# The opening and the closing of a one-core decoder layer: identity made on GpSimd, packed vectors on ScalarE's queue, large scalings and transposes behind the first rows, output as four pieces on two queues

## The chip, the cores and the metric

The kernel runs on one core of one Trainium2 chip. The metric is the device time of one execution in microseconds, the median of several runs. Engines are called as in the profile: PE (TensorE), DVE (VectorE), ACT (ScalarE), POOL (GpSimd) and SP (SyncE, which here does nothing but issue transfers). Transfers are also issued on ACT's queue.

## The reference, cut to what matters

One decoder layer on 256 tokens of width 1024, with weights in float32. The opening is the first half-FFN: a modulation vector comes from `c`, the rows of `x` are normed and modulated, and go through the gate and up projections.

```python
c_act = silu(c)
mod = c_act @ w_ada + b_ada                      # 1024 x 9216
sh1, sc1, g1, sh2, sc2, g2, sh3, sc3, g3 = split(mod, 9)
u = rmsnorm(x, norm_ff1) * (1 + sc1) + sh1
h = x + 0.5 * g1 * ((silu(u @ w_ff1_gate) * (u @ w_ff1_up)) @ w_ff1_down)
...                                              # token mixing (GLA and MoBA), second half-FFN
return rmsnorm(h, norm_final)                    # 256 x 1024
```

## The kernel before, in words

Each float32 product is made of three passes: weights and rows are both split into a high part (`hi`, `uh`: rounded by an ACT copy) and the remainder (`lo`, `ul`: a DVE subtraction), and hi*hi, hi*lo and lo*hi are added in PSUM. A matmul here is 128 x 128 weights against 256 tokens. All weights (140 MB) stream through eight raw buffers of 128 x 1024, issued on SP's queue in the order of use; a load waits for the release of a raw buffer by DVE, and each transfer counts on one of eight completion semaphores that are taken in turn, so that a transfer also waits for the eighth before it.

The opening works on eight blocks k of 128 input features. For each block come two pieces of the modulation weights (`a`, from `adal`) and two of the first eight columns of gate and up (`l`, from `lead`). What it does for block k, by the letters of the string `LEADING` (line 27), which is the order of program on every engine:

- `d`: a dot product of a modulation piece with `cact` on DVE (about 1.2 us), which gives the shift or the scale of block k
- `e`: ACT copies two turned blocks of x from PSUM to `xn`
- `u`, `c`, `v`: the modulated rows, their high part `uh` (ACT), their low part `ul` (DVE), both in the tile `ub`
- `h`, `r`: the high part of a weight piece (ACT) and its remainder (DVE)
- `x`: the 24 matmuls of a block with one of its two weight pieces

So blocks 0 and 1 together are 96 matmuls. Ahead of that stand, in program order: loads of the packed vectors `colt` (line 273, SP's queue), of x in two halves (line 276) and of the identity `ident` (line 279, ACT's queue); `csil` = silu(c) on ACT; eight transposes that spread `csil` over all partitions, and their two copies to `cact`; warm-up transposes of the identity (`keep_warm`, 22, and 8 and 7 later, by `WARM`); the squares of x (1024 and 512 wide on ACT, 512 on DVE), the mean, and the power -1/2 on POOL; then the scaling of x by it in pieces of 256 and 768 columns per half (`s`, `lead_scaled`), and the transposes of x (`t`, `lead_turned`), 4 for the first two blocks and 12 for the others, all of them ahead of the first matmul (line 690).

The constants of the token mixing (`mask`, `onehot`, `relt`, `wlr`, three of `tri`) and the transposed copy `xT` are written down later in the program (`mix_constants`, line 712, and line 736); a scheduler decides where their loads stand in SP's queue.

At the end the normed result is transposed (16 transposes into four PSUM banks), scaled by the inverse root mean square on its way out of PSUM, and written: five pieces, four transfers on SP's queue and one on ACT's (lines 1170 to 1173).

Of the kernel before, what the change touches and what calls it, by code (L numbers as in the profile page):

```python
# [11 lines left out]
F32R = mybir.dt.float32r  # L12
# [11 lines left out]
WARM = (22, 8, 7)  # L24
LOADS = """a00 a01 l00 l01 a10 a11 l10 l11 a20 a21 l20 l21 a30 a31 l30 l31 a40 a41 l40 l41 a50 a51 l50 l51 a60
         a61 l60 l61 a70 a71 l70 l71"""
LEADING = """u0 c0 h00 v0 r00 e1 h01 e2 e3 d10 r01 d11 h10 u1 c1 r10 v1 d20 h11 r11 x00 x01 d21 h20 u2 c2 r20 v2
# [48 lines left out]
def hybrid_layer(ctx: ExitStack, tc: tile.TileContext, x, xT, cols, ident_d, tri_d, mask_d, onehot_d,  # L76
# [196 lines left out]
    nc.sync.dma_start(colt, cols)  # L273
# [5 lines left out]
    nc.scalar.dma_start(ident, ident_d)  # L279
# [9 lines left out]
    in_order(True, vec, act, ten)  # L289
    csil = cst.tile([P, KD], F32, name="csil")  # L290
# [10 lines left out]
    pc = [bank(), bank()]  # L301
# [3 lines left out]
    warm = bank()  # L305

    def keep_warm(n):

        for _ in range(n):
            ten.transpose(warm[:, :P], ident, ident)  # L310

    keep_warm(WARM[0])

    sq, ssq = [mid([P, D]), mid([P, D])], row((P, 8), tag="tiny", bufs=4)
    act.activation(sq[0], xt[:, 0:D], AF.Square, accum_out=ssq[:, 0:1])
    act.activation(sq[1][:, 0:512], xt[:, D:D + 512], AF.Square, accum_out=ssq[:, 1:2])
# [299 lines left out]
    def lead_mm(k, w):  # L616
# [68 lines left out]
    def lead_xn(i):  # L685
# [7 lines left out]
    play(LEADING, {"d": lead_dot, "u": lead_u, "c": lead_uh, "v": lead_ul, "h": lead_high, "r": lead_low,  # L693
                   "e": lead_xn, "x": lead_mm, "A": stream.more})
# [587 lines left out]
```

## Time and profile before

| | |
|---|---|
| time, median of 3 runs | 568.15 us (567.98 to 568.35) |
| the profiled execution | 568.44 us, its span 566.7 us |
| PE busy | 556.5 us (98% of the span), 4757 matmuls |
| DVE busy | 442.1 us (78%) |
| ACT busy | 304.5 us (54%) |
| POOL busy | 10.8 us (2%) |
| mean granted clock of PE | 0.998 |

The span runs from the first to the last instruction of the profiled execution; the time is 1.74 us longer. Times below are microseconds from the start of the span. A row of the timeline merges instructions of one kind that follow each other: start, the time they took together, engine, line, operation, out<-in, shape, count, and in brackets the idle time of the engine before it and what ended it. Almost all instructions go through one recording helper and carry its line, L101, so they are told apart by the names of what they read and write. In those names `b` is a PSUM bank or the large buffer that holds x; `tiny` holds the mean and its inverse root; `raw` is a weight as loaded. Ends of matmuls are modelled.

### The profile page before, as it was taken

What the parts mean: (1) busy time and instruction counts of PE and PEld (TensorE: products, weight loads), DVE (VectorE), ACT (ScalarE), POOL (GpSimd) and SP (SyncE); (2) the same over time, 40 slices, a digit from 0 to 9 for tenths busy, and PEclk for the clock granted to TensorE, in tenths of its full rate; (3) what the DMA queues carried; (4) which work ended last, traced back from release to release, by engine and by line L of the source; (5) the groups of instructions that cost most, each with busy time, mean ns of one, the idle gap of its engine ahead of it and who ended that gap; (6) DMA issues with size and microseconds to landing.
All of it is one profiled execution on the core that took longest, in us unless ns stands there. A gap on an engine that the chain in (4) does not pass through costs nothing.

```text
span 566.7 us, 11731 instructions
## 1 busy us (share of the span) xinstructions
PE 556.5 (98%) x4757; PEld 550.1 (97%) x4757; DVE 442.1 (78%) x683; ACT 304.5 (54%) x484; POOL 10.8 (2%) x14
## 2 busy tenths in 40 slices
PE   7999999999999999999999999999999999999996
PEld 6999999999999999998999999999999999999995
DVE  5999888788887896899998979789874656665535
ACT  5557763354455667843864543576644454455424
POOL 0000000000000110000001000000000000000000
PEclk9999999999999999999999999999999999999999
DMA  8999789999998636454499788834896566775102
GB/s 320 401 408 408 250 274 377 407 385 345 300 387 296 216 106 225 156 183 150 121 313 381 256 284 282 283 128 120 265 360 218 191 199 216 260 246 178 56 1 74
DMA packets 39799, 142.03 MB, mean 251 GB/s; under 512 B 4621, under 2 KB 5186, under 8 KB 39618
## 3 DMA queue, kind: packets, MB, share of 16 engines
q1 hardware_dynamic: 39282, 140.44, 71.2%
q8 instruction: 37, 0.61, 0.4%
q0 software_dynamic: 176, 0.53, 0.3%
q10 hardware_dynamic: 288, 0.33, 0.2%
q14 instruction: 16, 0.13, 0.1%
HBM read 140.22 MB, written 1.05 MB: 249 GB/s over the span
## 4 chain that ended last, share of the span: by engine, by line
PE 59%; issue 32%; DVE 5%; DMA 2%; ACT 1%; POOL 0%; SPq 0%; POOLq 0%; DVEq 0%
PE b L101 59%; DVE lo L101 2%; DMA raw<-in_lead 1%; DVE b L101 1%; DVE s L101 1%; DMA b<-in_x 1%; DVE raw L101 0%; POOL tiny L361 0%; ACT b L101 0%; ACT hi L101 0%; POOLq L1277 0%; DVEq L1277 0%; ACT ub L101 0%; DVE tiny L101 0%; SPq L276 0%
## 5 line engine op out<-in xcount | busy, mean ns | idle before, releaser
L101 PE MATMUL b<-ub,hi 128*128 128x256 f32 (+1 forms) x1920 | 329.9, 278 | 0.3 <-DVE ub L101 0.3
L101 PEld LDWEIGHTS b<-ub,hi 128*128 128x128 f32 x1920 | 288.6, 188 | 1.9 <-issue 1.0
L101 DVE TENSOR_TENSOR lo<-raw,hi 128x1024 fp32r<-128x1024 f32 (+2 forms) x189 | 225.4, 1218 | 65.8 <-ACT hi L101 64.6
L101 PE MATMUL b<-ub,lo 128*128 128x256 f32 (+1 forms) x960 | 262.4, 277 | 0.0
L101 ACT ACTIVATE hi<-raw 128x1024 fp32r<-128x1024 f32 (+2 forms) x189 | 193.8, 1049 | 69.9 <-issue 32.0
L101 PEld LDWEIGHTS b<-ub,lo 128*128 128x128 f32 x960 | 178.9, 188 | 0.0
L101 PE MATMUL b<-s,hi 128*128 128x256 f32 x960 | 164.6, 276 | 0.0
L101 PEld LDWEIGHTS b<-s,hi 128*128 128x128 f32 x960 | 144.7, 188 | 0.0
L101 PE MATMUL b<-s,lo 128*128 128x256 f32 x480 | 132.7, 276 | 0.0
L101 PEld LDWEIGHTS b<-s,lo 128*128 128x128 f32 x480 | 90.1, 188 | 0.0
L101 DVE SCALAR_TENSOR_TENSOR raw<-raw,cact 128x1024 f32<-128x1024 f32 (+1 forms) x64 | 75.9, 1221 | 0.0
L101 ACT ACTIVATE s<-m 128x256 fp32r<-128x256 f32 x52 | 21.4, 417 | 77.9 <-DVE m L101 77.8
L101 ACT ACTIVATE sg<-b 128x256 f32<-128x256 f32 x46 | 17.1, 379 | 47.8 <-PE b L101 45.9
L101 DVE TENSOR_TENSOR s<-m,s 128x256 fp32r<-128x256 f32 x52 | 21.8, 424 | 20.6 <-ACT s L101 20.3
L101 DVE TENSOR_TENSOR m<-sg,b 128x256 f32<-128x256 f32 x43 | 17.9, 418 | 13.5 <-ACT sg L101 13.4
L101 ACT ACTIVATE s<-b 128x256 f32<-128x256 f32 (+5 forms) x34 | 14.5, 474 | 25.1 <-PE b L101 22.0
L101 PE MATMUL b<-hi,ub 128*128 128x264 f32 (+1 forms) x96 | 21.7, 321 | 0.0
L101 PEld LDWEIGHTS b<-hi,ub 128*128 128x128 f32 x96 | 15.8, 188 | 1.2
L101 PE MATMUL b<-lo,ub 128*128 128x264 f32 (+1 forms) x48 | 15.4, 321 | 0.0
L101 DVE SCALAR_TENSOR_TENSOR b<-b,mods,b 128x256 f32<-128x256 f32 x24 | 10.6, 479 | 4.5 <-PE b L101 4.5
L361 POOL TENSOR_TENSOR tiny<-tiny,mhalf 128x2 f32<-128x2 f32 (+1 forms) x5 | 7.1, 1418 | 364.4 <-DVE tiny L101 364.4
L101 ACT ACTIVATE sq<-b 128x256 f32<-128x256 f32 x24 | 9.2, 407 | 5.6 <-DVE b L101 5.2
(124 smaller groups left out, 278.7 us busy)
## 6 DMA issues: line engine op xcount, KB each, us to landing
raw<-in_gu SPq DMA_DIRECT2D x72, 512.0 KB, 5.7
raw<-in_ada SPq DMA_DIRECT2D x56, 512.0 KB, 6.2
raw<-in_dn SPq DMA_DIRECT2D x44, 512.0 KB, 6.1
raw<-in_win SPq DMA_DIRECT2D x24, 512.0 KB, 4.8
raw<-in_adal SPq DMA_DIRECT2D x16, 513.0 KB, 8.2
raw<-in_lead SPq DMA_DIRECT2D x16, 512.0 KB, 8.0
raw<-in_gbr SPq DMA_DIRECT2D x16, 512.0 KB, 6.1
raw<-in_wout SPq DMA_DIRECT2D x8, 512.0 KB, 6.1
```

Of the source, the lines that this page charges most:

```text
L101: x = getattr(self.engine, op)(*args, **kw)
L361: nc.gpsimd.tensor_tensor(out=rs[:, :n], in0=ms[:, :n], in1=mhalf[:, :n], op=ALU.pow)
```

## The change

The identity is no longer loaded: GpSimd clears it and a select on the diagonal sets the ones; DVE casts a second copy, `ident_r`, to fp32r. The packed vectors go to ACT's queue. Warming up is now a plain matmul of `ident_r` with itself, 10 ahead of the transposes of `csil` and 24 behind them, and nothing later. ACT squares both halves of x whole. Ahead of the first matmul remain the two small scalings, four transposes and one copy to `xn`; the large scalings (`s11` on DVE, `s01` on ACT) and the 12 transposes (`t11`, `t01`) move into `LEADING`, behind the 16 matmuls of block 0 that need only the high part of the weights (`x00`); its 8 matmuls with the remainder follow as `y00`. The eight accumulation banks are handed out in another order. The output is two pieces of 512 columns per half, one on each queue. In the excerpt a line of three dots marks what is left out.

```diff
-WARM = (22, 8, 7)
+WARM = (10, 24)
...
-LEADING = """u0 c0 h00 v0 r00 e1 h01 e2 e3 d10 r01 d11 h10 u1 c1 r10 v1 d20 h11 r11 x00 x01 d21 h20 u2 c2 r20 v2
+LEADING = """u0 c0 s11 h00 v0 r00 x00 s01 t11 t01 y00 h01 e1 e2 e3 d10 r01 d11 h10 u1 c1 r10 v1 d20 h11 r11 x01 d21 h20 u2 c2 r20 v2
...
-    nc.sync.dma_start(colt, cols)
+    nc.scalar.dma_start(colt, cols)
...
-    nc.scalar.dma_start(ident, ident_d)
+    nc.gpsimd.memset(ident, 0.0)
+    nc.gpsimd.affine_select(out=ident, in_=ident, pattern=[[-1, P]], compare_op=ALU.not_equal, fill=1.0, base=0,
+                            channel_multiplier=1)
...
+    ident_r = cst.tile([P, P], F32R, name="ident_r")
+    vec.tensor_copy(ident_r, ident)
+
+    def keep_warm(n):
+        for _ in range(n):
+            ten.matmul(warm[:, :P], ident_r, ident_r, start=True, stop=True)
...
-            ten.transpose(warm[:, :P], ident, ident)
...
-    act.activation(sq[0], xt[:, 0:D], AF.Square, accum_out=ssq[:, 0:1])
-    act.activation(sq[1][:, 0:512], xt[:, D:D + 512], AF.Square, accum_out=ssq[:, 1:2])
...
-    vec.scalar_tensor_tensor(sq[1][:, 512:], xt[:, D + 512:2 * D], 1.0, xt[:, D + 512:2 * D], op0=ALU.mult,
-                             op1=ALU.mult, accum_out=ssq[:, 2:3])
-    vec.tensor_tensor(out=ssq[:, 1:2], in0=ssq[:, 1:2], in1=ssq[:, 2:3], op=ALU.add)
+    for t in range(2):
+        act.activation(sq[t], xt[:, t * D:(t + 1) * D], AF.Square, accum_out=ssq[:, t:t + 1])
...
-    def lead_mm(k, w):
+    def lead_mm(k, w, low=None):
...
         for at, part, r in order:
+            if low not in (None, part):
+                continue
...
-    play("s00 t00 s10 t10 s01 w1 e0 s11 t01 t11 w2", {
-        "s": lead_scaled, "t": lead_turned, "e": lead_xn, "w": lambda i: keep_warm(WARM[i])})
-    lead_banks = [bank() for _ in range(LEAD)]
+    play("s00 t00 s10 t10 e0", {"s": lead_scaled, "t": lead_turned, "e": lead_xn})
+    free = [bank() for _ in range(LEAD)]
+
+    lead_banks = [free[i] for i in (0, 1, 2, 3, 5, 6, 4, 7)]
...
-    pieces = [scaled(vec, 0, 512, 256), scaled(act, 0, 0, 512), scaled(vec, 0, 768, 256), scaled(vec, 1, 512, 512)]
-    for to, src in pieces:
-        nc.sync.dma_start(to, src)
-    nc.scalar.dma_start(*scaled(act, 1, 0, 512))
+    for t in range(2):
+        nc.scalar.dma_start(*scaled(act, t, 0, 512))
+        nc.sync.dma_start(*scaled(vec, t, 512, 512))
```

How the built programs stand, first PE from its warm-up to its first matmul of block 0, before (`b_106` takes the warm-up, `b_1_72` is x, `b_159` to `b_163` its turned blocks, `ub_75` the modulated rows):

```order
L101 MATMUL b_106<-ident 128x128 x22
L101 MATMUL b_159<-ident,b_1_72 128x128 x4
L101 MATMUL b_106<-ident 128x128 x8
L101 MATMUL b_160<-ident,b_1_72 128x128 x2
L101 MATMUL b_162<-ident,b_1_72 128x128 x2
L101 MATMUL b_163<-ident,b_1_72 128x128 x2
L101 MATMUL b_160<-ident,b_1_72 128x128 x2
L101 MATMUL b_162<-ident,b_1_72 128x128 x2
L101 MATMUL b_163<-ident,b_1_72 128x128 x2
L101 MATMUL b_106<-ident 128x128 x7
L101 MATMUL b_202<-ub_75,hi_213 128x256
```

PE in the changed kernel from its first instruction to the first matmul of block 0 (`b_89` takes the warm-up, `b_174` the turned blocks 0 and 1):

```order
L101 MATMUL b_89<-ident_r 128x128 x10
L101 MATMUL b_90<-ident,csil 128x128 x4
L101 MATMUL b_91<-ident,csil 128x128 x4
L101 MATMUL b_89<-ident_r 128x128 x24
L101 MATMUL b_174<-ident,b_1_72 128x128 x4
L101 MATMUL b_188<-ub_75,hi_200 128x256
```

And PE in the changed kernel at the end of the 16 matmuls of `x00` (`b_175` to `b_178` are the turned blocks 2 to 7, `lo_201` is the remainder of block 0's first weight piece):

```order
L101 MATMUL b_189<-ub_75,hi_200 128x256
L101 MATMUL b_191<-ub_75,hi_200 128x256
L101 MATMUL b_175<-ident,b_1_72 128x128 x2
L101 MATMUL b_177<-ident,b_1_72 128x128 x2
L101 MATMUL b_178<-ident,b_1_72 128x128 x2
L101 MATMUL b_175<-ident,b_1_72 128x128 x2
L101 MATMUL b_177<-ident,b_1_72 128x128 x2
L101 MATMUL b_178<-ident,b_1_72 128x128 x2
L101 MATMUL b_188<-ub_75,lo_201 128x256
L101 MATMUL b_190<-ub_75,lo_201 128x256
```

The 12 transposes of x now stand between the matmuls with the high part of the weights and those with the remainder, and no warm-up stands behind the first four transposes.

SP's queue before, around the loads for block 2 (`raw_237` and `raw_292` are its modulation pieces, `raw_295` and `raw_305` its weights):

```order
L163 DMA raw_153<-in_lead 128x1024
L163 DMA raw_237<-in_adal 128x1026
L163 DMA raw_292<-in_adal 128x1026
L163 DMA raw_295<-in_lead 128x1024
L163 DMA raw_305<-in_lead 128x1024
L163 DMA raw_307<-in_adal 128x1026
```

The same place in the changed kernel (`raw_261` and `raw_292` are the modulation pieces of block 2, `raw_295` and `raw_305` its weights):

```order
L163 DMA raw_168<-in_lead 128x1024
L163 DMA raw_261<-in_adal 128x1026
L163 DMA raw_292<-in_adal 128x1026
L722 DMA mask<-in_mask 128x448
L722 DMA wide_836<-in_onehot 32x384
L722 DMA relt<-in_relT 32x4
L163 DMA raw_295<-in_lead 128x1024
L163 DMA raw_305<-in_lead 128x1024
```

Three loads of the token mixing's constants have come in ahead of the first weight piece of block 2; before, `mask` stood 39 places further back. The load of `xT` also stands 12 transfers earlier than it did, between two of the `tri` loads.

ACT's queue before, from the scaling of x to the rows of block 1 (`hi_213`, `hi_221` and `hi_229` are the high parts of the weights, `b_9_138` is `xn`):

```order
L101 ACTIVATE b_1_72<-b_1_72,tiny_157 128x256 x2
L101 ACTIVATE b_1_72<-b_1_72,tiny_157 128x768
L101 ACTIVATE b_9_138<-b_159 128x512
L101 ACTIVATE ub_75<-b_9_138,gemv 128x256
L101 ACTIVATE hi_213<-raw_143 128x2x256 x2
L101 ACTIVATE b_9_138<-b_160 128x512
L101 ACTIVATE hi_221<-raw_145 128x2x512
L101 ACTIVATE b_9_138<-b_162 128x512
L101 ACTIVATE b_9_138<-b_163 128x512
```

The same place in the changed kernel (`b_9_153` is `xn`):

```order
L101 ACTIVATE b_1_72<-b_1_72,tiny_172 128x256 x2
L101 ACTIVATE b_9_153<-b_174 128x512
L101 ACTIVATE ub_75<-b_9_153,gemv 128x256
L101 ACTIVATE hi_200<-raw_158 128x2x256 x2
L101 ACTIVATE b_1_72<-b_1_72,tiny_172 128x768
L101 ACTIVATE hi_244<-raw_160 128x2x512
L101 ACTIVATE b_9_153<-b_175 128x512
L101 ACTIVATE b_9_153<-b_177 128x512
L101 ACTIVATE b_9_153<-b_178 128x512
```

The wide scaling now comes behind the high part of block 0's first weight piece, and the second weight piece ahead of the three copies to `xn`.

## Rows read from the trace of the kernel before

**Rows 1.** The page, part 1: busy time, share of the span and instructions of each engine.

```profile
PE 556.5 (98%) x4757; PEld 550.1 (97%) x4757; DVE 442.1 (78%) x683; ACT 304.5 (54%) x484; POOL 10.8 (2%) x14
```

**Rows 2.** What PE waited for in the whole span: us in total, times, longest.

```profile
PE b L101 <- ACT b L101: 1.0, 1, 1.0
PE b L101 <- DVE ub L101: 0.3, 1, 0.3
```

**Rows 3.** The chain of waits that ended last, in order of time, from the last load of the opening on: start, us, what.

```profile
14.00 8.42 DMA raw<-in_lead
...
22.44 1.07 ACT hi L101
...
24.76 0.35 DVE ub L101
...
25.15 216.59 PE b L101 x1875
```

**Rows 4.** Busy time by stretch, two in the warm-up and two at the end: stretch, its length, busy us and count of PE, PEld (weight loads), DVE, ACT and POOL, granted clock of PE, share of the 16 DMA engines, GB/s.

```profile
5.00:7.40 2.40, 2.40 (x13) 2.40 (x12) 0.89 (x2) 1.34 (x3) 0.00 (x0) 1.00 1.02 414
7.80:8.60 0.80, 0.80 (x10) 0.76 (x7) 0.55 (x5) 0.13 (x2) 0.07 (x1) 1.00 0.99 354
561.00:564.00 3.00, 0.44 (x5) 0.20 (x2) 1.25 (x3) 0.97 (x2) 0.00 (x0) 1.00 0.58 212
564.00:566.70 2.70, 0.00 (x0) 0.00 (x0) 0.00 (x0) 0.00 (x0) 0.00 (x0) 0.51 0.41 153
```

**Rows 5.** The timeline from 9 to 17 us.

```profile
9.27 1.74 ACT L101 ACTIVATE b<-b,tiny 128x256 f32<-128x256 f32 x3 [1.34 <-POOL tiny L361]
...
9.83 0.84 PE L101 MATMUL b<-ident,b 128*128 128x128 f32 x4 [1.03 <-ACT b L101]
...
10.91 0.57 ACT L101 ACTIVATE b<-b 128x512 f32<-128x512 f32 x1
...
10.92 0.62 DVE L101 TENSOR_SCALAR b<-b,tiny 128x768 f32<-128x768 f32 x1
...
11.38 1.47 PE L101 MATMUL b<-ident,b 128*128 128x128 f32 x12
...
11.52 0.60 ACT L101 ACTIVATE ub<-b,gemv 128x256 fp32r<-128x256 f32 x1
...
12.03 1.14 ACT L101 ACTIVATE hi<-raw 128x512 fp32r<-128x512 f32 x2
...
12.69 0.93 PE L101 MATMUL b<-ident 128*128 128x128 f32 x7
...
13.37 2.10 PE L101 MATMUL b<-ub,hi 128*128 128x256 f32 x16
...
16.31 1.06 ACT L101 ACTIVATE hi<-raw 128x1024 fp32r<-128x1024 f32 x1 [0.75 <-DMA raw<-in_lead]
```

**Rows 6.** Transfers, by what they load: queue, count, KB each, median us from issue to landing.

```profile
mask<-in_mask SPq DMA_DIRECT2D x1, 224.0 KB, 3.9
...
ident<-in_ident ACTq DMA_DIRECT2D x1, 64.0 KB, 2.2
...
wide<-in_onehot SPq DMA_DIRECT2D x1, 48.0 KB, 4.7
```

**Rows 7.** The timeline from 0 to 9 us, and at the end POOL's longest small instruction.

```profile
0.73 0.10 POOL L283 MEMSET mhalf<- 128x8 f32 x1 [0.29 <-POOLq L1269]
...
0.74 0.39 SPq L273 DMA_DIRECT2D colt<-in_cols  x1
...
1.18 0.90 SPq L276 DMA_DIRECT2D b<-in_x  x2
...
2.83 0.21 ACT L101 ACTIVATE csil<-colt 128x8 f32<-128x8 f32 x1 [0.36 <-DMA colt<-in_cols]
...
3.09 1.97 PE L101 MATMUL b<-ident,csil 128*128 128x128 f32 x8 [3.09 <-ACT csil L101]
...
4.85 3.95 PE L101 MATMUL b<-ident 128*128 128x128 f32 x22
...
5.09 0.69 DVE L101 COPY cact<-b 128x512 f32<-128x512 f32 x1 [0.16 <-PE b L101]
...
7.21 0.69 DVE L101 SCALAR_TENSOR_TENSOR s<-b 128x512 f32<-128x512 f32 x1 [1.42 <-DMA b<-in_x]
...
8.21 0.17 DVE L101 TENSOR_SCALAR tiny<-tiny 128x2 f32<-128x2 f32 x1
...
8.49 1.32 DVE L101 SCALAR_TENSOR_TENSOR raw<-raw,colt,cact 128x1026 f32<-128x1026 f32 x1
...
8.53 0.70 POOL L361 TENSOR_TENSOR tiny<-tiny,mhalf 128x2 f32<-128x2 f32 x1 [7.70 <-DVE tiny L101]
...
303.45 2.55 POOL L361 TENSOR_TENSOR tiny<-tiny,mhalf 128x8 f32<-128x8 f32 x1 [100.98 <-DVE tiny L101]
```

**Rows 8.** The timeline of the last results and of the output, and the time to landing of the pieces of 256 KB on either queue.

```profile
561.42 2.12 SPq L1172 DMA_DIRECT2D out<-b  x4
...
560.71 1.27 ACT L101 ACTIVATE b<-b,tiny 128x512 f32<-128x512 f32 x2 [1.34 <-POOL tiny L361]
...
562.00 0.36 ACTq L1173 DMA_DIRECT2D out<-b  x1
...
560.71 1.53 DVE L101 TENSOR_SCALAR b<-b,tiny 128x256 f32<-128x256 f32 x3 [0.81 <-POOL tiny L361]
...
out<-b SPq DMA_DIRECT2D x2, 256.0 KB, 2.4
...
out<-b ACTq DMA_DIRECT2D x1, 256.0 KB, 2.6
```

More of the change, by code (lines that the diff above doesn't have):

```diff
@@ L75, in hybrid_layer @@
 @with_exitstack
-def hybrid_layer(ctx: ExitStack, tc: tile.TileContext, x, xT, cols, ident_d, tri_d, mask_d, onehot_d,
+def hybrid_layer(ctx: ExitStack, tc: tile.TileContext, x, xT, cols, tri_d, mask_d, onehot_d,
                  relT, wlr, adal, ada, lead, gu1, dn1, win, gv, mv, gbr, wout, gu2, dn2, out):
@@ L289, in hybrid_layer @@
     in_order(True, vec, act, ten)
+    warm_up = [bank() for _ in range(3)]
+    warm, pc = warm_up[0], warm_up[1:]
+    ident_r = cst.tile([P, P], F32R, name="ident_r")
[3 more added lines that the diff above has]
+            ten.matmul(warm[:, :P], ident_r, ident_r, start=True, stop=True)
     csil = cst.tile([P, KD], F32, name="csil")
@@ L300, in hybrid_layer @@
     vec.memset(cact[:, D:], 1.0)
-    pc = [bank(), bank()]
+    keep_warm(WARM[0])
     for i in range(KD):
         ten.transpose(pc[i // 4][:, blk(i % 4)], csil[:, i:i + 1].to_broadcast([P, P]), ident)
-    warm = bank()
-    def keep_warm(n):
-        for _ in range(n):
-            ten.transpose(warm[:, :P], ident, ident)
-    keep_warm(WARM[0])
-    sq, ssq = [mid([P, D]), mid([P, D])], row((P, 8), tag="tiny", bufs=4)
-    act.activation(sq[0], xt[:, 0:D], AF.Square, accum_out=ssq[:, 0:1])
-    act.activation(sq[1][:, 0:512], xt[:, D:D + 512], AF.Square, accum_out=ssq[:, 1:2])
+    keep_warm(WARM[1])
     for i in range(2):
         vec.tensor_copy(cact[:, i * 512:(i + 1) * 512], pc[i])
-    vec.scalar_tensor_tensor(sq[1][:, 512:], xt[:, D + 512:2 * D], 1.0, xt[:, D + 512:2 * D], op0=ALU.mult,
-                             op1=ALU.mult, accum_out=ssq[:, 2:3])
-    vec.tensor_tensor(out=ssq[:, 1:2], in0=ssq[:, 1:2], in1=ssq[:, 2:3], op=ALU.add)
+    sq, ssq = [mid([P, D]), mid([P, D])], row((P, 8), tag="tiny", bufs=4)
+    for t in range(2):
+        act.activation(sq[t], xt[:, t * D:(t + 1) * D], AF.Square, accum_out=ssq[:, t:t + 1])
     def ada_dot(raw, s, j):
@@ L689, in hybrid_layer @@
     lead_dot(0, 1)
-    play("s00 t00 s10 t10 s01 w1 e0 s11 t01 t11 w2", {
-        "s": lead_scaled, "t": lead_turned, "e": lead_xn, "w": lambda i: keep_warm(WARM[i])})
-    lead_banks = [bank() for _ in range(LEAD)]
+    play("s00 t00 s10 t10 e0", {"s": lead_scaled, "t": lead_turned, "e": lead_xn})
+    free = [bank() for _ in range(LEAD)]
+    lead_banks = [free[i] for i in (0, 1, 2, 3, 5, 6, 4, 7)]
     play(LEADING, {"d": lead_dot, "u": lead_u, "c": lead_uh, "v": lead_ul, "h": lead_high, "r": lead_low,
-                   "e": lead_xn, "x": lead_mm, "A": stream.more})
+                   "e": lead_xn, "s": lead_scaled, "t": lead_turned, "y": lambda k, w: lead_mm(k, w, 1),
+                   "x": lambda k, w: lead_mm(k, w, None if k or w else 0), "A": stream.more})
     h = big()
@@ L1218, in _constants @@
         onehot[_buckets()[dist], 127 + dist] = 1.0
-    return (np.eye(P, dtype=np.float32), tri.astype(np.float32), np.stack(masks, 1).astype(np.int32), onehot)
+    return (tri.astype(np.float32), np.stack(masks, 1).astype(np.int32), onehot)
 def _packed(i):
@@ L1229, in _packed @@
     d["cols"] = _c(np.concatenate(vec).reshape(N_COLS, P).T)
-    d["ident"], d["tri"], d["mask"], d["onehot"] = _constants()
+    d["tri"], d["mask"], d["onehot"] = _constants()
     d["relT"] = _c(w["rel_bias"].T)
@@ L1256, in _packed @@
     return d
-_INS = ["x", "xT", "cols", "ident", "tri", "mask", "onehot", "relT", "wlr", "adal", "ada", "lead", "gu1", "dn1", "win",
+_INS = ["x", "xT", "cols", "tri", "mask", "onehot", "relT", "wlr", "adal", "ada", "lead", "gu1", "dn1", "win",
         "gv", "mv", "gbr", "wout", "gu2", "dn2"]
```

## The prediction

> **What bounds the kernel now.** I read the page first, then what TensorE waits for, then the chain that ended last, then the opening and the closing engine by engine. The page has PE busy for 98% of the span [rows 1]. Its only sizable waits lie at the two ends; the last of the opening is 0.3 us for `ub` from VectorE [rows 2], and in the chain of waits that place is 25.15 us, from which PE's own work runs for 216.59 us without a piece of another engine [rows 3]. From there on one thing follows: the rest of the time is PE's instruction count, which the change leaves alone. So the time can move at two places only: when PE can take up block 2 of the first projection without another wait (25.15 us now), and how long the last output transfer takes after the last result.
>
> What holds block 2 back, read backwards in the same chain [rows 3]: its low rows (`ub`, 24.76) stand in VectorE's queue behind the remainder of a weight tile (`lo`), that waits for ScalarE's copy of it (22.44), and that for the weight's landing, asked for at 14.00 and there at 22.4. That transfer took 8.4 us because the DMA engines are full: share 1.02 and 414 GB/s already at 5 us [rows 4]. PE itself was done with blocks 0 and 1 almost as early: it began them at 13.37 [rows 5], they are 96 matmuls, and at the chain's pitch of 216.59/1875 = 0.1155 us that is 11.1 us, so 24.5. Two things bind within 0.7 us of each other: PE's own work and the weights' arrival. A change that helps one of them gains at most the small distance to the other.
>
> **The change, part by part, up to 25.15.**
>
> *Identity.* The load of 64 KB on ScalarE's queue goes [rows 6]; a memset, a select on GpSimd and a cast on VectorE come. No row has the select. From below: GpSimd's small memset is 0.10 us; from above: its longest instruction on few elements is 2.55 us [rows 7]. With the memset over at about 0.9 (0.73 plus some 0.2), the identity is there between 1.0 and 3.5 us. I take 1.1 us for the select, in between, since it computes nothing like the power of the 2.55 us row but touches sixteen times as many elements as the memset's row. That gives 2.0, and the cast 2.3. What must wait for it: ten warm-up matmuls (1.1 to 2.1 us, each between half and the whole of the 0.2 us that a transpose takes early in the span, [rows 4]) and the eight transposes of `csil`, after which 2.7 us pass until both copies into `cact` are done (3.09 to 5.09 + 0.69, [rows 7]). So `cact` is ready between 6.1 and 7.1. Its first reader starts at 8.49 today and about 8.1 in the changed kernel (below): 1 us of cover, gone when the identity comes after 3.0 to 4.0.
>
> *Packed vectors on ScalarE's queue.* On SP's queue x then goes out at 0.74, where `colt` was, and not at 1.18 [rows 7]: all loads start 0.44 us sooner. `colt` takes the place of the identity on the other queue and now shares the engines with x from the start. `csil` may slip from 2.83 [rows 7] by up to 1 us (x's half megabyte takes 1.27 us at 414 GB/s); the same cover holds.
>
> *Squares.* VectorE loses a square of 0.69 us and a small add; ScalarE squares two whole halves. The second begins when x has landed, 7.21 today [rows 7], about 6.6 then (0.44 and the identity's 0.16 us sooner), takes 1.06 (ScalarE's 128x1024 pass, [rows 5]) and 0.2 for its sum: 7.9 against the 8.21 of today's scaling of the mean. The power (0.70) ends near 8.9 and not 9.24; the first dot starts near 8.1 and not 8.49, with its weights 0.6 us sooner.
>
> *Order.* Today ScalarE scales three pieces (9.27, 1.74 us), PE transposes 4, 12 and warms itself with 8 and 7 more, and the first matmul of block 0 comes at 13.37, when the weight copy begun at 12.03 had long given its first half at 12.6 [rows 5]: PE was still in the last warm-up. Then: the two small scalings 8.95 to 9.85, four transposes to 10.35, `xn` 10.4 to 10.95 (0.57), the rows' high half 11.0 to 11.6 (0.60), the first half of the weights 12.1. VectorE's 768-wide scaling (0.62) now stands behind `u`, and the low rows are ready at 12.3. First matmul: 12.2, so **1.2 us earlier**. But the 12 transposes (1.47 us, [rows 5]) now stand among the matmuls: 12.2 + 11.1 + 1.5 = 24.8 for the end of block 1, against 24.5. What was gained by starting early is spent where it was saved.
>
> Behind the moved transposes hang ScalarE's three copies to `xn`; they end near 16.6, so its next weight copy, which today starts at 16.31 on its landing [rows 5], comes at 16.5. That passes to VectorE's queue as at most 0.15 us.
>
> *Weights of block 2.* The order shows a transfer that the diff doesn't: mask, one-hot and a tiny third load now stand on SP ahead of this weight. They are 224 + 48 KB [rows 6], 0.67 us at 414 GB/s. Sum for the landing: -0.44 (x sooner) - 0.16 (64 KB less) + 0.67 = **+0.07**. Those loads also take three of the eight turns in which SP reuses its completion semaphores, so SP asks for later weights up to 2 us later; with 8.4 us from asking to landing and 1.27 us for each, six or seven large ones are queued now and three or four would still be, which I price at nothing. If that cover fails, the engines run dry for part of a transfer of 1.27 us. Block 2's low rows come at 25.2 to 25.3, after PE is free at 24.8: **opening +0.1 us**. From then on a block is fed every 4 x 1.27 = 5.1 us and worked off in 48 x 0.1155 = 5.5, so PE falls behind its feed and nothing is late next. The transfer of `xT` (1 MB), also moved forward, lies beside PE work that is some tiles ahead.
>
> **Closing.** Today SP issues four pieces one behind the other, 561.42 to 563.54, while VectorE is through at 562.24 and ScalarE at 561.98 [rows 8]. Then each queue has two: ScalarE 560.71 to 561.4, issue 0.36, second piece to 562.5, issue at 562.5, landing 2.6 later at 565.1; VectorE 560.71, 561.4 to 562.1, issue near 562.2, landing 564.6. Today's last issue begins near 562.8 (four in 2.12 us, the last the longest) and lands 2.4 later, 565.2. ScalarE's issue in the middle costs its second piece 0.36. **Closing -0.3 us** (0 to -0.7).
>
> **Sum.** +0.1 - 0.3 = -0.2 us on the profiled execution's 568.44. That one lies 0.29 above the median of the runs, 568.15; on the median: **568.0 us**.
>
> **The clock, weighed.** In 5.00 to 7.40 PE loads 12 weights in 2.40 us, in 7.80 to 8.60 seven in 0.80 [rows 4]: 0.20 against 0.114 us each, the lower level (1.2 GHz) and the higher, although the granted column prints 1.00 for both. It had done nothing but transposes since 3.09. At the other end the granted clock was 1.00 until 564.00 and 0.51 behind it, with the last transposes over at about 561.4 [rows 4]. A gap of 1.03 us before 9.83 didn't lower it [rows 5]. The Trainium skill (TensorE: Matmul & The Clock Gate, Part 4: PE-mode transpose) says that transposes don't count as work for that clock; this trace disagrees, since by that rule block 0's first 16 matmuls would have taken 16 x 0.23 = 3.7 us, and they took 2.10 [rows 5]. By the rule only the new plain warm-up matmuls would help, and the sum would gain; by the rows it doesn't.
>
> **The rivals.**
>
> *Clock lost in the opening.* Warm-up now ends by about 7.8, and until 12.2 PE has only four transposes, where today 8 and 7 more fill in. If the clock is at its lower level when block 0 begins and stays there 2 to 4 us, half of that is lost: blocks 0 and 1 end at 25.8 to 26.8, the copies behind the moved transposes slip alike, and block 2 waits to 25.7 to 26.7. Opening +0.5 to +1.5, total 568.4 to 569.4; with a longer low stretch 570. For it: the fall at 564.00, 2.6 us after the last work. Against: four transposes lie between, and the gap of 1.03 was harmless. It decides from 1 us of low clock on.
>
> *Identity late (the other side).* From an identity at 3.0 to 4.0 on, each further us moves `cact`, the dots and block 0 by a whole one. At the 2.55 us row it comes at 3.5 and costs 0 to 0.5. But that row is for 8 elements a partition, and from the 0.70 us of 2 elements it grows by 0.31 us an element [rows 7], so that it doesn't bound 128 of them well: a select of twice the row, 5.1 us, gives the identity at 6.0 and `cact` at 10.1 to 11.1, 2 to 3 us late, and 570 to 571. Speaking for it: today's first real GpSimd instruction runs at 8.53, so any preparation was hidden. Against: it then took only 0.70 us, and a compare is far from a power. The Trainium skill (GPSIMD Engine Reference, 2.1 Instruction dispatch) gives about 6 us for the first call of freshly loaded code, by which the total would be some 572, an estimate; no run here shows it yet.
>
> *A real gain.* If the weights land sooner than summed (the small loads slip into idle turns), PE's own 24.8 binds, or 24.2 if block 0 is begun half a microsecond sooner still: 0.4 to 1 off in the opening, with up to 0.7 at the end: 566.5 to 567.4.
>
> **How the numbers follow.** Forecast (568.0, own range 567.5 to 568.4) 0.50; clock lost 0.28; identity late 0.12; real gain 0.10. About 0.2% (1.1 us) is what a measurement can tell from no change. Slower: all of the late identity and a quarter of the lost clock, 0.19. Faster: six tenths of the gain, 0.06. The same: 0.75. The range reaches from 567.2 to 570.0, leaving out a late identity and the outer end of the gain.
>
> **What would show it.** First block-0 matmul near 12.2; twelve transposes behind 16 matmuls; block 2 taken up at 25.2 +/- 0.3 with the wait still on VectorE's low rows; the weight landing at 22.5; the select about 1 us; the last issue on ScalarE at 562.5 less the shift. Weight loads of block 0 at twice the pitch, or `cact` after 8.1, would make it wrong.

## The result, and the profile after

The changed kernel takes 573.38 us (median of 12 runs, 568.94 to 573.63) against 568.30 (12 runs): ratio 1.0079, interval 1.0064 to 1.0094, **0.8% slower**. The forecast was 568.0, no change, with a range to 570.0. The profiled execution took 573.62 us with a span of 571.8, 5.1 more than that of before. (A ratio, here and below, is not the quotient of the medians beside it.) One execution of the kernel without its 24 warm-ups, 810.98 us at a mean granted clock of 0.657, is left out of what follows.

In the profiled execution all of it lies in the opening. First the timeline of PE, changed kernel (start, us, what, count; in brackets the idle time ahead and what ended it):

```profile
1.62 2.40 PE L101 MATMUL b<-ident_r 128*128 128x128 f32 x10 [1.62 <-DVE ident_r L101]
5.49 1.94 PE L101 MATMUL b<-ident,csil 128*128 128x128 f32 x8 [1.47 <-ACT csil L101]
7.08 5.36 PE L101 MATMUL b<-ident_r 128*128 128x128 f32 x24
12.24 1.07 PE L101 MATMUL b<-ident,b 128*128 128x128 f32 x4
15.15 3.78 PE L101 MATMUL b<-ub,hi 128*128 128x256 f32 x16 [1.84 <-ACT hi L101]
18.73 2.66 PE L101 MATMUL b<-ident,b 128*128 128x128 f32 x12
21.14 1.16 PE L101 MATMUL b<-ub,lo 128*128 128x256 f32 x8
22.14 1.98 PE L101 MATMUL b<-ub,hi 128*128 128x256 f32 x16
```

The 24 warm-ups run from 7.08 to 12.24, 0.215 us each, and x's first four transposes follow them at once. Block 0 begins at 15.15 (13.37 in [rows 5]), its 16 matmuls take 3.78 us (2.10 there), and the second weight of block 0 is begun at 22.14; in the kernel before, the same group stands here:

```profile
16.21 1.98 PE L101 MATMUL b<-ub,hi 128*128 128x256 f32 x16
```

So block 0 begins 1.78 later, and from there to this group pass 6.99 us instead of 2.84, 4.15 more. The kernel before then needs 25.15 - 16.21 = 8.94 us for 72 matmuls that take 8.16 at 0.1133 us each (the 24 from 18.03 on take 2.72): 0.78 of small waits, the one of [rows 2] among them, which the changed kernel, being late, doesn't have. 1.78 + 4.15 - 0.78 = 5.15, the 5.1 of the spans.

The level of the clock is read from the pitch of the weight loads, the time from one load to the next (columns as in [rows 4]):

```profile
7.40:12.20 4.80, 4.80 (x25) 4.80 (x24) 3.17 (x6) 0.93 (x3) 1.66 (x1) 1.00 1.00 397
15.60:18.50 2.90, 2.90 (x15) 2.90 (x15) 2.90 (x5) 1.79 (x3) 0.00 (x0) 1.00 1.01 413
21.20:24.00 2.80, 2.80 (x27) 2.80 (x26) 0.77 (x1) 2.77 (x6) 0.00 (x0) 1.00 1.02 406
```

24 loads in 4.80 us and 15 in 2.90: 0.20 and 0.19 us each, the lower level (1.2 GHz). Only from 21.2 on it is 0.108. In the kernel before it rose within the warm-up, ahead of 7.8 [rows 4]. The granted column prints 1.00 throughout, as it did there ahead of the first change.

Two more places. The packed vectors land late, and `csil` behind them (chain, then timeline):

```profile
0.73 4.38 DMA colt<-in_cols
...
5.49 7.84 PE b L101 x36
```

```profile
5.13 0.21 ACT L101 ACTIVATE csil<-colt 128x8 f32<-128x8 f32 x1 [2.68 <-DMA colt<-in_cols]
10.08 0.91 ACT L101 ACTIVATE b<-b,tiny 128x256 f32<-128x256 f32 x2 [2.66 <-POOL tiny L364]
13.35 0.60 ACT L101 ACTIVATE b<-b 128x512 f32<-128x512 f32 x1 [2.36 <-PE b L101]
```

`csil` starts at 5.13 (2.83 in [rows 7]), and from 5.49 to 13.33 the chain is PE's own work, the warm-up in it. x's small pieces are scaled by 10.99, but PE transposes them only from 12.24, since it is still in its warm-up; `xn` at 13.35 waits for that.

And the closing:

```profile
565.81 0.69 ACT L101 ACTIVATE b<-b,tiny 128x512 f32<-128x512 f32 x1 [1.34 <-POOL tiny L364]
566.59 1.11 SPq L1179 DMA_DIRECT2D out<-b  x2
567.67 0.34 ACTq L1178 DMA_DIRECT2D out<-b  x1
```

From the first result instruction to the end of the span pass 571.8 - 565.81 = 5.99 us; before, 566.7 - 560.71 = 5.99 [rows 8]. The closing gave nothing, and the whole loss is PE's late start and its slow block 0.

### The profile page after: what moved, and what is told of

Its sections match the earlier page's. It is cut to its first block, busy times and chain, and to the rows that moved or that the text cites. A ratio compares the mean times of both kernels' runs of the same rounds, so it can differ in the third digit from the quotient of the medians.

```text
span 571.8 us, 11720 instructions
## 1 busy us (share of the span) xinstructions
PE 561.1 (98%) x4754; PEld 554.9 (97%) x4754; DVE 440.7 (77%) x680; ACT 304.5 (53%) x484; POOL 12.2 (2%) x16
## 4 chain that ended last, share of the span: by engine, by line
PE 62%; issue 31%; DVE 4%; DMA 1%; ACT 1%; POOL 0%; POOLq 0%; ACTq 0%; DVEq 0%
PE b L101 62%; DVE b L101 1%; DVE lo L101 1%; DVE s L101 1%; DMA colt<-in_cols 1%; DVE raw L101 0%; ACT b L101 0%; POOL tiny L364 0%; POOLq L1283 0%; ACT ub L101 0%; ACT hi L101 0%; ACTq L1178 0%; ACT csil L101 0%; DVE tiny L101 0%; DVEq L101 0%
## 5 line engine op out<-in xcount | busy, mean ns | idle before, releaser
L101 DVE SCALAR_TENSOR_TENSOR b<-b,mods,b 128x256 f32<-128x256 f32 x24 | 10.6, 477 | 4.5 <-PE b L101 4.5
```

What stands on the lines that cost most here:

```text
L101: x = getattr(self.engine, op)(*args, **kw)
```

## The experiments

Theory A: back-to-back plain fp32r matmuls do not raise the clock, as the fp32 transposes of before did. Theory B: the hole of 1.47 us at 4.02, left by the late vectors, kept it low. Theory C: the twelve transposes moved among the matmuls are the loss by themselves. Theory D came later, from the run with both repairs and the one with the order alone: the new order leaves PE at rest ahead of block 0, and that takes the clock away. Medians stand beside 568.4 for the kernel before, which was run with each group of them. It has such executions too, though few: six of the 94 in the four groups took 569.66 to 571.01 us at a mean granted clock of 0.996. In the code excerpts a line of three dots marks what is left out.

**The changed kernel, warming with transposes.**

```diff
-    ident_r = cst.tile([P, P], F32R, name="ident_r")
-    vec.tensor_copy(ident_r, ident)
...
-            ten.matmul(warm[:, :P], ident_r, ident_r, start=True, stop=True)
+            ten.transpose(warm[:, :P], ident, ident)
```

> The changed kernel with its 10 and 24 warm-up matmuls written as transposes of the fp32 identity again; nothing else differs. Theory A (which instruction warms: back-to-back plain fp32r matmuls of 128 columns leave the clock low, fp32 transposes raise it): the clock is up before block 0 begins, its 24 matmuls and the 12 transposes among them take 4.3 us and not 6.99, and the second half of the 24 warm-ups runs at 0.11 us instead of 0.213, so that the first matmul comes at 14 and not 15.15; less up to 1 us for the wait at block 2 that returns: 569.5 to 570.7 us. Theory B (the idle stretch 4.02 to 5.49 in the warm-up, left by the late packed vectors, keeps the clock low whatever fills the rest): no change, 573.4. Theory C (the transposes moved among the matmuls are the loss, the clock is not): no change, 573.4.

Measured: 569.34 us (1.0018, interval 1.0009 to 1.0028). 4.0 of the 5.0 us are back by the kind of the warm-up instruction alone, so B and C are not the main cause: the hole and the moved transposes are still there. (Nine of the ten executions took 568.94 to 569.87 us; one took 571.34, at a granted clock of 0.995.)

```profile
7.12 3.90 PE L101 MATMUL b<-ident 128*128 128x128 f32 x24
10.86 0.60 PE L101 MATMUL b<-ident,b 128*128 128x128 f32 x4
13.30 2.09 PE L101 MATMUL b<-ub,hi 128*128 128x256 f32 x16 [1.84 <-ACT hi L101]
15.23 1.47 PE L101 MATMUL b<-ident,b 128*128 128x128 f32 x12
17.50 1.98 PE L101 MATMUL b<-ub,hi 128*128 128x256 f32 x16
```

```profile
7.40:9.30 1.90, 1.90 (x11) 1.90 (x10) 1.78 (x3) 0.27 (x1) 0.71 (x1) 1.00 0.94 352
9.50:10.80 1.30, 1.30 (x14) 1.30 (x13) 1.22 (x4) 0.44 (x2) 0.00 (x0) 1.00 1.02 413
```

Ten loads in 1.90 us, then 13 in 1.30: the clock rises at 9.4, among the 24 transposes. Block 0 begins 1.85 sooner, and from there to the group at 17.50 pass 4.20 us and not 6.99; 1.85 + 2.79 = 4.64, the difference of the spans (571.8 and 567.2). Of the 4.15 us that this stretch had grown by, the clock is 2.79; the other 1.36 are the moved transposes, which stood ahead of block 0 before.

**The packed vectors first on SyncE's queue**, warm-up still plain.

```diff
-    nc.scalar.dma_start(colt, cols)
+    nc.sync.dma_start(colt, cols)
```

> The changed kernel with the packed vectors back at the head of SyncE's queue, ahead of x; nothing else differs. All theories: the vectors land near 2.8 and not 5.1, the eight transposes of csil follow the first ten warm-ups without a gap, and the 24 warm-ups end near 10.8 and not 12.24, so x's transposes and block 0 begin 1.2 to 1.4 us sooner. Theory A (plain matmuls don't raise the clock): pitch of block 0 stays at 0.213 us, 572.0 to 572.4 us. Theory B (the gap kept the clock low): nine microseconds without a gap raise it before block 0, 568.5 to 569.5 us.

Measured: 571.62 us (1.0038, 1.002 to 1.0056).

```profile
13.47 3.78 PE L101 MATMUL b<-ub,hi 128*128 128x256 f32 x16 [1.84 <-ACT hi L101]
```

The hole is gone; PE works from 1.62 to 11.6 without one, and in the profiled execution (571.79 us) block 0's first 16 matmuls still take 3.78 us from 13.47 on. The hole is not what kept the clock low there. But only three of the five executions are like it: the two others took 569.50 and 569.55 us at a mean granted clock of 0.995 against 0.998, times at the upper end of the range of B. No trace of them is kept; that the clock rose in them and fell again is only argued. In the three, what the late vectors cost by themselves is the shift of the start, 15.15 to 13.47, and 1.8 us of the time.

**The kernel before, warming with plain fp32r matmuls.**

```diff
+    ident_r = cst.tile([P, P], F32R, name="ident_r")
+    vec.tensor_copy(ident_r, ident)
...
-            ten.transpose(warm[:, :P], ident, ident)
+            ten.matmul(warm[:, :P], ident_r, ident_r, start=True, stop=True)
```

> The kernel before with its 37 warm-up transposes (22, 8, 7) written as plain matmuls of an fp32r copy of the same identity (one cast on VectorE more). Theory A (plain matmuls don't raise the clock): no rise near 7.6; the 16 transposes of x and 15 warm-ups from 9.8 on take 0.213 us each and not 0.109, block 0 begins near 16.5 and not 13.37, and runs at the low level itself for some microseconds: 570.5 to 573 us. Theories B and C (the gap, or the moved transposes): nothing of either is in this kernel, 568.3 us.

Measured: 569.39 us (1.0018, 1.0008 to 1.0027): slower, as A has it and B and C don't, but by 1.0 and not by 2 to 4.6.

```profile
5.00:9.40 4.40, 4.40 (x23) 4.40 (x22) 2.58 (x7) 2.71 (x7) 0.70 (x1) 1.00 0.90 340
9.60:14.20 4.60, 4.60 (x24) 4.60 (x24) 4.50 (x10) 2.70 (x6) 0.00 (x0) 1.00 1.02 409
15.70:17.40 1.70, 1.70 (x17) 1.70 (x16) 1.70 (x2) 1.70 (x3) 0.00 (x0) 1.00 1.03 420
```

22 loads in 4.40 us and 24 in 4.60, the lower level until 14.2; but by block 0 (15.67) it is up. Between lie the twelve fp32 transposes of x (11.99 to 14.4) and the last seven warm-ups. The old order has those transposes ahead of block 0, the new one behind its 16 matmuls. That would be why the same plain warm-up costs little in the old order and much in the new; no run takes it apart.

**The changed kernel without its 24 plain warm-ups.**

```diff
-WARM = (10, 24)
+WARM = (10, 0)
```

> The changed kernel without its 24 plain warm-up matmuls (ten before csil's transposes, none behind). If these 24 raise no clock and only stand in front of x's transposes: block 0 begins as soon as x's first pieces are scaled, near 13.9 instead of 15.15, at the same low pitch of 0.213: 572.0 to 572.6 us. If they were of use to the clock at all: later than 573.4, since the low stretch lasts longer.

Measured: 571.21 us (median of six; 1.0046, 1.0032 to 1.006), 2.2 less than with them and 0.8 below the range expected.

```profile
10.62 1.12 PE L101 MATMUL b<-ident,b 128*128 128x128 f32 x4 [3.22 <-ACT b L101]
13.58 3.78 PE L101 MATMUL b<-ub,hi 128*128 128x256 f32 x16 [1.84 <-ACT hi L101]
17.16 2.26 PE L101 MATMUL b<-ident,b 128*128 128x128 f32 x12
```

Block 0 begins 1.57 sooner at the same pitch: in the profiled executions the 24 did nothing for the clock and stood in front of x's transposes.

**Both repairs in the changed kernel**: transposes as warm-up, and vectors first.

> The changed kernel with both repairs: the warm-ups as fp32 transposes and the packed vectors back at the head of SyncE's queue. Theory A with its second half (the 24 warm-ups stand in front of x's transposes, and the late vectors hold the warm-ups): csil near 2.9, the 24 transposes end near 9 instead of 10.86 (the run with transposes alone), so x's scaling (9.4 to 9.9) sets block 0, which begins near 12.4 and not 13.30: PE's own part ends 0.9 us sooner, near 24.8, where block 2's rows (25.0 to 25.4) begin to bind: 568.4 to 568.9 us against 569.34 of the transposes alone. If the late vectors matter only through the clock: no gain on 569.34.

Measured: 569.73 us (1.0016, 1.0003 to 1.0029), no gain on the transposes alone, although in the profiled execution block 0 began at 12.04 instead of 13.30 and the time was 568.02, below the kernel before.

```profile
12.04 2.10 PE L101 MATMUL b<-ub,hi 128*128 128x256 f32 x16 [2.07 <-ACT hi L101]
```

The ten executions divide by the granted clock: the three at 568.02 to 568.67 have 0.997 or 0.998, the seven at 569.72 to 570.89 have 0.993 to 0.996. In those seven the clock had gone again for some microseconds; where, no kept trace shows. This miss led to theory D.

**The new order alone, in the kernel before** (first 22 warm-up transposes, identity, queues and closing kept; those of 8 and 7 gone, as the new order has it).

```diff
-LEADING = """u0 c0 h00 v0 r00 e1 h01 e2 e3 d10 r01 d11 h10 u1 c1 r10 v1 d20 h11 r11 x00 x01 d21 h20 u2 c2 r20 v2
+LEADING = """u0 c0 s11 h00 v0 r00 x00 s01 t11 t01 y00 h01 e1 e2 e3 d10 r01 d11 h10 u1 c1 r10 v1 d20 h11 r11 x01 d21 h20 u2 c2 r20 v2
...
-    play("s00 t00 s10 t10 s01 w1 e0 s11 t01 t11 w2", {
-        "s": lead_scaled, "t": lead_turned, "e": lead_xn, "w": lambda i: keep_warm(WARM[i])})
...
+    play("s00 t00 s10 t10 e0", {"s": lead_scaled, "t": lead_turned, "e": lead_xn})
...
```

> The kernel before with the new order alone: two small scalings and four transposes of x ahead, x00, then the other twelve transposes, y00; no warm-up of 8 and 7 in front of block 0; the first 22 warm-up transposes, identity, queues and closing stay. By the sum on record: first matmul 12.2, and the twelve transposes add 1.3 to 1.5 behind it, so block 1 ends near 24.8 and block 2 is taken up at 25.2: 568.3 to 568.6 us. Theory C (the moved transposes are the loss by themselves): 571 or more. A clock that falls where PE rests between the first 22 warm-ups and block 0 (8.5 to 12.2 with four transposes in it): pitch 0.213 at block 0, 569.5 to 571.

Measured: 570.16 us (1.0022, 1.0007 to 1.0036). PE's timeline, then its stretches:

```profile
4.79 4.12 PE L101 MATMUL b<-ident 128*128 128x128 f32 x22
10.51 0.84 PE L101 MATMUL b<-ident,b 128*128 128x128 f32 x4 [1.60 <-ACT b L101]
13.19 3.78 PE L101 MATMUL b<-ub,hi 128*128 128x256 f32 x16 [1.84 <-ACT hi L101]
```

```profile
8.00:11.30 3.30, 1.70 (x12) 1.06 (x10) 3.05 (x7) 1.52 (x4) 0.70 (x1) 1.00 1.00 397
11.40:18.10 6.70, 4.91 (x23) 4.91 (x24) 6.11 (x11) 3.99 (x6) 0.00 (x0) 0.50 1.02 384
18.30:22.00 3.70, 3.70 (x34) 3.70 (x33) 0.96 (x3) 3.43 (x7) 0.00 (x0) 1.00 1.02 417
```

Here the granted column itself shows it: full until 11.3, half from 11.4 to 18.1, full again. Ahead of the fall PE had rested for 1.60 us and done four transposes, until 11.35; the second rest, 1.84 us, begins with the fall and cannot be its cause. All ten executions have a mean of 0.992 to 0.996.

**Both repairs, and the rest filled** with 18 transposes behind x's first four (the two repairs are left out of the excerpt).

```diff
-WARM = (10, 24)
+WARM = (10, 24, 18)
...
-    play("s00 t00 s10 t10 e0", {"s": lead_scaled, "t": lead_turned, "e": lead_xn})
+    play("s00 t00 s10 t10 w2 e0", {"w": lambda i: keep_warm(WARM[i]), "s": lead_scaled, "t": lead_turned, "e": lead_xn})
...
```

> The changed kernel with both repairs (fp32 transposes as warm-up, packed vectors first on SyncE's queue), and 18 more warm-up transposes between the first four transposes of x and block 0's first matmul, where PE rests from 10 to 12 in the run with both repairs. Theory D (the new order takes the clock away again in that rest: the run with the order alone showed the clock up at 7.96, down at 11.37 and up again at 18.20, and the times of the run with both repairs lie between 568.02 and 570.89): the clock stays up in every execution, block 0's first 16 matmuls take 2.1 us, and all times lie near the best of that run: 568.0 to 568.4, with no execution over 569. If the rest isn't the reason: times between 568.0 and 570.9 as before, median near 569.7.

Measured: 568.72 us (1.0005, 0.9996 to 1.0014), eleven executions between 568.32 and 568.93, none over 569 and none at a granted clock under 0.998.

```profile
9.65 0.84 PE L101 MATMUL b<-ident,b 128*128 128x128 f32 x4 [0.83 <-ACT b L101]
10.32 2.13 PE L101 MATMUL b<-ident 128*128 128x128 f32 x18
12.43 2.09 PE L101 MATMUL b<-ub,hi 128*128 128x256 f32 x16
```

The spread of 2.9 us is down to 0.6: work in place of the rest keeps the clock, as D has it. The median is 0.3 above what I expected at most; block 0 began at 12.43, behind the 18, and not at 12.04.

**The new order alone, its rests filled**, the 18 in the same place.

```diff
-WARM = (22, 8, 7)
+WARM = (30, 18)
...
```

> The kernel before with the new order alone, as in the run of that kind (570.16 us), but 30 instead of 22 warm-up transposes ahead of x and 18 behind x's first four, so that PE has no long rest ahead of block 0. Theory D: no fall of the clock at 11.4, block 0's first 16 matmuls take 2.1 and not 3.78 us, and the rest of the new order costs what the sum on record gave it, a start sooner by some and twelve transposes behind it: 568.3 to 568.9. Theory C (the moved transposes lose the time by themselves): 569.5 or more with the clock up.

Measured: 568.43 us (1.0004, 0.9995 to 1.0013), 1.7 less than the order alone.

```profile
9.26 0.84 PE L101 MATMUL b<-ident,b 128*128 128x128 f32 x4 [0.34 <-ACT b L101]
12.45 2.15 PE L101 MATMUL b<-ub,hi 128*128 128x256 f32 x16 [0.38 <-ACT hi L101]
```

The two rests are 0.34 and 0.38 us, and the 16 matmuls run at the higher level. C falls: with the clock held up, the order costs and gains nothing that can be told, as the sum had it.

**The changed kernel, warming with plain fp32 matmuls** (identity with itself, 4 and 10).

```diff
-            ten.matmul(warm[:, :P], ident_r, ident_r, start=True, stop=True)
+            ten.matmul(warm[:, :P], ident, ident, start=True, stop=True)
```

> The changed kernel with its warm-ups as plain fp32 matmuls of the identity with itself (no fp32r copy, not written as transposes), 4 and 10 instead of 10 and 24, since one may take longer. Which instruction raises the clock: if fp32 does, transposed or not, the clock is up before block 0 as in the run with transposes (rise at 9.4 there), 569.0 to 570.5 us; if only transposing does, it stays low through block 0 as in the changed kernel, 572 to 573.5 us.

Measured: 570.67 us (1.0034, 1.002 to 1.0047), six executions from 568.62 to 571.33. Between the two numbers expected, and the profile says why:

```profile
13.44 3.34 PE L101 MATMUL b<-ub,hi 128*128 128x256 f32 x16 [1.84 <-ACT hi L101]
16.58 1.88 PE L101 MATMUL b<-ident,b 128*128 128x128 f32 x12
```

```profile
10.70:13.90 3.20, 1.36 (x13) 1.12 (x11) 1.63 (x4) 2.50 (x6) 0.00 (x0) 1.00 1.03 418
14.10:17.40 3.30, 3.30 (x17) 3.30 (x17) 3.30 (x6) 1.59 (x2) 0.00 (x0) 0.50 1.02 415
17.50:20.00 2.50, 2.50 (x24) 2.50 (x23) 0.74 (x2) 1.94 (x4) 0.00 (x0) 1.00 1.01 407
```

Eleven loads in 1.12 us: the clock is up by 10.7, so plain fp32 raises it too, and the missing transposing is not what fails. Behind the rest of 1.84 us ahead of 13.44 it is down, from 14.1 to 17.4, and then up again. In that low stretch PE did little but block 0's own matmuls, which are fp32r too but 256 wide, with x's next transposes only from 16.58 on. So fp32r as such is not shown to be what fails either: which property of the 128-wide fp32r warm-up leaves the clock low, no run separates.

**The old order with the new identity and queue** (18 warm-up transposes ahead of `csil`'s, 12 behind, 8 in x's gap, none at the end).

```diff
-WARM = (22, 8, 7)
+WARM = (18, 12, 8)
...
-    nc.sync.dma_start(colt, cols)
+    nc.scalar.dma_start(colt, cols)
...
-    nc.scalar.dma_start(ident, ident_d)
+    nc.gpsimd.memset(ident, 0.0)
+    nc.gpsimd.affine_select(out=ident, in_=ident, pattern=[[-1, P]], compare_op=ALU.not_equal, fill=1.0, base=0,
+                            channel_multiplier=1)
...
-    play("s00 t00 s10 t10 s01 w1 e0 s11 t01 t11 w2", {
+    play("s00 t00 s10 t10 s01 w2 e0 s11 t01 t11", {
...
```

> The kernel before with the identity made on GpSimd and the packed vectors on ScalarE's queue, in the old order; 18 warm-up transposes before and 12 behind csil's eight, 8 in the gap behind the first four transposes of x, none after the last twelve. Closing as before. Theory A: the clock is up before 9; loads are asked for 0.44 us sooner and 64 KB less stands ahead, so block 2's weights land 0.6 us sooner and block 0 begins near 12.3 instead of 13.37; PE's own end of block 1 then 23.4, block 2 taken up at 24.5 on VectorE's rows: 0.6 us less than before, 567.7 us. If the loads gain nothing (the late vectors slow x as much as they let it go sooner): 568.3.

Measured: 569.29 us (1.0008, 0.9997 to 1.0019), a miss: neither the 567.7 nor the 568.3 expected. In the profiled execution the clock is up at 7.0 and stays (in five of the ten the mean is 0.994 to 0.997). But `colt` is late, so VectorE copies `cact` until about 7.9 and comes to its square of x only at 7.89 (7.21 in [rows 7]), and the power took 1.6 us:

```profile
7.89 0.68 DVE L101 SCALAR_TENSOR_TENSOR s<-b 128x512 f32<-128x512 f32 x1
9.20 1.60 POOL L364 TENSOR_TENSOR tiny<-tiny,mhalf 128x2 f32<-128x2 f32 x1 [7.90 <-DVE tiny L101]
...
11.40 0.84 PE L101 MATMUL b<-ident,b 128*128 128x128 f32 x4 [2.85 <-ACT b L101]
```

Block 0 begins at 14.26. The earlier x is lost to the later vectors and the longer power. The last row matters for theory D: PE rested 2.85 us here and the clock stayed, block 0's 16 matmuls taking 2.14 us, while it fell behind 1.60 us in the run with the order alone. The length of a rest alone does not decide.

**The old order, lean**: identity on GpSimd as in the last diff, the last 7 warm-ups gone, all else as before.

```diff
-WARM = (22, 8, 7)
+WARM = (22, 8)
...
-    play("s00 t00 s10 t10 s01 w1 e0 s11 t01 t11 w2", {
+    play("s00 t00 s10 t10 s01 w1 e0 s11 t01 t11", {
...
```

> The kernel before in its old order, with the identity made on GpSimd and without the last 7 warm-up transposes ahead of block 0; queues and closing as before. Two things bind within 0.7 us of each other in the kernel before, PE's own work and block 2's rows, and this helps the first: block 0 begins near 12.6 and not 13.37, with the clock up (the twelve transposes of x end just ahead of it); PE then waits near 0.9 us instead of 0.3 for block 2's rows, which come 0.16 us sooner because 64 KB less stands ahead of their weights: 568.1 to 568.4 us, no difference that can be told. If PE's own work alone binds: 567.6 to 567.8.

Measured: 568.63 us (0.9998, 0.9989 to 1.0008). Block 0 begins at 12.43 instead of 13.37, and block 2 is taken up no sooner (chain):

```profile
13.78 8.77 DMA raw<-in_lead
...
24.89 0.35 DVE ub L101
...
25.28 8.77 PE b L101 x75
```

And PE's timeline, with its waits below:

```profile
18.74 1.22 PE L101 MATMUL b<-ub,hi 128*128 128x256 f32 x8 [0.54 <-ACT ub L101]
...
PE b L101 <- DVE ub L101: 0.3, 1, 0.3
```

PE gives the 0.9 us back, but not where I expected it: the wait for block 2's low rows is 0.3 us, as in [rows 2], and not 0.9; 0.54 go for block 1's high rows, and the rest in a slightly slower run of matmuls. The weight's arrival binds, and there was nothing to win in the opening on PE's side. The landing didn't come 0.16 sooner for the 64 KB less: 13.78 + 8.77 = 22.55, against 22.42 in [rows 3].

**The new closing alone, in the kernel before.**

```diff
-    pieces = [scaled(vec, 0, 512, 256), scaled(act, 0, 0, 512), scaled(vec, 0, 768, 256), scaled(vec, 1, 512, 512)]
...
+    for t in range(2):
+        nc.scalar.dma_start(*scaled(act, t, 0, 512))
+        nc.sync.dma_start(*scaled(vec, t, 512, 512))
```

> The kernel before with only the new closing (four pieces of 512 columns, two on ScalarE's queue and two on SyncE's). The prediction on record had -0.3 us for it: 568.0. From the two traces, where from the first result instruction to the end of the span 5.99 us pass in both kernels: 568.3, a difference of 0.1 or less.

Measured: 568.58 us (1.0004, 0.9994 to 1.0013): no difference.

## Why the prediction was wrong, step by step

**The clock, weighed: the step that failed.** The rows showed that fp32 transposes raise the clock, and from that I concluded that the opening would be warm. But the change took 37 of these away and put plain fp32r matmuls in their place, of which no row said anything; I counted them as warm-up because they bear that name. So the sum ran blocks 0 and 1 at 0.1155 us a matmul and put the clock at nothing. The runs: 24 of them in a row at 0.215 us leave the clock low, and block 0's first 16 matmuls take 3.78 us instead of 2.10; the same number of transposes raise it, 4.0 us between the two. The prediction had set a rule of the Trainium skill (TensorE: Matmul & The Clock Gate, Part 4: PE-mode transpose), that transposes don't count, against the trace. The run with transposes in the changed kernel disagrees with that rule more plainly still: the clock rose at 9.4 among them. My reading of it was right; what I drew from it was not, since the remark that "only the new plain warm-up matmuls would help" was dropped without the other question, whether they help at all.

**Warm-up, a second step, mis-sized.** From that came the second error. I had the warm-up over by 7.8, which is 24 at the higher level behind an early `csil`. At the lower one they take 5.2 us, end at 12.24, and stand ahead of x's transposes, ready at 10.99. Without them 2.2 us are back. The first matmul was to come at 12.2 and came at 15.15; with transposes and early vectors it came at 12.04 in the profiled execution.

**Clock lost in the opening** was a rival at 0.28, by PE's rest ahead of block 0. That mechanism exists, in the order alone: 1.7 us, the 570 that I gave it for a longer low stretch and more than its 0.5 to 1.5. What spoke against it, that a gap of 1.03 us did no harm in [rows 5], was one gap; in the order alone the clock fell behind a rest of 1.60 and four transposes. A rest does not always do it: 1.84 us took the clock in the profiled run with plain fp32 and not in the one with transposes, and 2.85 us left it in the old order with the new identity. What decides between them is open. In the profiled execution of the changed kernel the rest could do nothing, since there was no high level to lose; it shows once the warm-up is repaired.

**Squares.** The mean was scaled at 8.07, near the 7.9 of the sum, but the power took 1.66 us and not 0.70, so that x was scaled from 10.08 and not from 8.95. Here the warm-up until 12.24 hid it; in the run without the 24 warm-ups x's transposes waited for that scaling, until 10.62.

**Packed vectors.** The slip was put at up to 1 us and was 2.3 (`csil` 5.13 for 2.83). The cover for `cact` just held: its first reader started at 8.19, near the 8.1 of the sum. But the slip also moved the 24 warm-ups behind `csil`'s transposes and x's transposes behind those, which I had not followed; that moved block 0 by 1.7 us. The load was bounded by x's half megabyte, 1.27 us, and slipped by more. The Trainium skill (DMA: Bandwidth & Descriptors, Queues, rings and completion order) says that a DMA engine takes turns between queues packet by packet. 4.4 us instead of some 2.1 to landing for 56.5 KB agree with engines that are shared; how the turns went, no run here shows.

**Identity.** Right side, and near the lower bound: the select took 0.29 us, where the rows gave 0.10 to 2.55 and I took 1.1, and it was over at 1.30. The rival of a late identity is refuted. The Trainium skill (GPSIMD Engine Reference, 2.1 Instruction dispatch) has about 6 us for a first call of freshly loaded code; no run here shows such a price, and the select at 1.01 did not pay it.

**Order, weights, closing.** With the clock held up the order is worth 0.0 (forecast +0.1, the two parts of it -1.2 and +1.5); the lean old order shows that block 2's weights bind at 25.2 to 25.3, as the first part of the prediction had it. The closing was put at -0.3 and was 0. The two landings that the prediction itself works out, 565.1 against 565.2, give only -0.1; and the last issue begins 1.86 us behind the first result and not 1.8, and lands 2.8 later and not 2.6.

What stays open: why a median run lost 5 us and one of the twelve 0.6, and two of the five with early vectors 1.1. Traces of these executions aren't there; a clock that rose ahead of block 0 in them would give this, but it is only argued. Open too is which property of the warm-up matmul leaves the clock low, and which rest takes it.

## What to carry to other kernels

When a warm-up is rewritten, ask of the new instruction, not of the word, whether it raises the clock: read the pitch of weight loads ahead of and behind it. A warm-up is also work in a queue: count it at the low level, and see what stands behind it. And where an order saves time by letting TensorE rest ahead of the main work, price the rest with the clock, not with the idle time, and look at many executions, since one trace can miss it. Filling the rest with fp32 transposes took 1.7 us off the order alone; with both repairs it took 1.0 us off the median and most of the spread, although block 0 then began 0.4 later than in the best execution without them.

## What the runs showed of the hardware that I had not expected

- Plain fp32r matmuls of 128x128 back to back (0.215 us) left the clock at the lower level in the profiled executions (7.08 to 12.24; in the run with early vectors 1.62 to 10.6, with eight fp32 transposes among them). It rose among plain fp32 matmuls (by 10.7) and among fp32 transposes (at 9.4).
- A granted column of 1.00 can stand beside the lower level: until the first change that the record holds it prints 1.00 whatever the pitch (0.20 us a load from 7.4 to 12.2 in the changed kernel).
- The clock fell with no rest longer than 1.60 us since its rise, and four transposes behind that rest (the order alone, 11.4), and outlived one of 2.85 (the old order with the new identity).
- GpSimd's power of 2 elements a partition took 0.70 to 0.72 us in most profiles, and 1.60 to 1.76 in four (the changed kernel, the one with `WARM = (10, 0)`, the one with plain fp32, the old order with the new identity and queue), all with the identity made on GpSimd and the vectors on ScalarE's queue; but the run with transposes had both too, and took 0.71. What decides it is open.
- A small load beside x's megabyte took 4.4 us to land, and some 2.1 ahead of it.
